# Layer 1's feed-forward output product as seven block products instead of eight

## The chip, the core and the metric

The kernel runs on one core of a Trainium2 chip. The metric is the device time of one launch in microseconds (us), the median of repeated runs. On the core TensorE (PE) multiplies, VectorE (DVE) and ScalarE (ACT) do elementwise work, GpSimd (POOL) a little more, and SyncE (SP) issues the DMAs. Every engine takes its own instructions strictly in the order in which they stand in the program.

## What is computed

A two-layer backbone over 1024 latent tokens and 256 context tokens, in fp32. Layer 0 mixes by a gated convolution and a chunked gate, layer 1 by attention; each ends in a SwiGLU feed-forward part. The change concerns the feed-forward part of layer 1, for the latent tokens:

```
def _swiglu(h, w_in, w_out):
    gt, up = jnp.split(h @ w_in, 2, axis=-1)
    return (jax.nn.silu(gt) * up) @ w_out
x = _post_norm(x, _swiglu(_modulate(x, m_lat[3], m_lat[4]), ffn_w_in[l], ffn_w_out[l]),
               m_lat[5], ln_g[l, 1], ln_b[l, 1])
# _post_norm(x, y, gate, g, b) = _layernorm(ALPHA * x + gate * y, g, b)
# w_in 1024 x 5632, w_out 2816 x 1024; 1024 tokens
```

## The kernel before

A matrix product in fp32 is made of three matmuls (`mm3`, L89 to L92): both operands are split into a rounded part (hi, a cast on ACT, L201) and the rest (lo, a subtraction on DVE, L202), and hi·hi, hi·lo and lo·hi are added up in a PSUM bank. One matmul is 128x128 by 128x512. Its stationary side is called a here, its moving side b.

The feed-forward input product, `ffn_in2` (L547), is a seven-product scheme already: for each of the 22 inner blocks j (128 wide) it makes seven products W[n] by H, four `mm3` each, and combines them on DVE. Its result for block j, two 128x512 tiles `d` and `a` (the two token halves), goes to the DRAM tensor `act_d` (L635, L638). After each second block `step` lets one piece of the background job `bg_ada` run: the adaLN vectors, two loads of `ada_w` and two multiply-adds on DVE (L128) a piece, a sum over partitions on POOL after each fourth.

The output product, `ffn_out2` (L641), is a plain blocked one. Two halves `kb` of 11 inner blocks; in each, for the two output halves h, the weights are loaded and split (`sw` to `w2`, 22 buffers), and with h = 0 the activations come back from `act_d` (`raw`, L656) and are split into `aT`. Then two groups of four token tiles, with the inner block outside and the tile inside, so that four PSUM banks are filled together; only the last group goes tile by tile (`end`). The first half's banks are copied out on ACT (L695); in the second half DVE adds them, multiplies by the gate and adds the residual (L701 to L703, L699). That is 22 x 8 x 2 `mm3`, 1056 matmuls. The end of the program (L1177 to L1186) is a layer norm of the eight token tiles on DVE: two BN_STATS (L208), an aggregate, a power on POOL, two instructions with the mean (L1181), two with the scale (L1184), and the stores.

The order of each engine's instructions is fixed when the program is built: a scheduler plays the program through with its own model of time, and each engine's queue is the order in which things came up there. Buffers (`U`: 61 tiles of 128x512; `w2`: 22; `sw`: 4) are handed out in that order too. All DMAs stand in SP's queue.

## Time and profile before

| | us |
|---|---|
| median of 3 runs | 2629.03 (2627.96 to 2629.47) |
| the profiled execution, whole | 2629.6 |
| its span, first to last instruction | 2627.7 |
| layer 1's `ffn_in2` in the span | about 1952 to 2369 |
| layer 1's `ffn_out2`, first to last matmul | about 2369 to 2608 |
| after the last matmul | 2608 to 2627.7 |

Busy shares over the span: PE 97%, weight loads 81%, DVE 70%, ACT 36%, POOL 12%. The mean granted TensorE clock is 0.987 of full speed. A matmul's own duration in the rows (0.39 us) is longer than the distance to the next one, since matmuls overlap: for PE the distance from start to start counts.

### The profile page before, as it was taken

The page shows a single profiled execution, that of the slowest core. Times are in us where ns is not written, and L with a number is a line of the kernel's source. Part 1 is how long each engine was busy: PE and PEld are TensorE (multiplying, and loading weights), DVE is VectorE, ACT ScalarE, POOL GpSimd, SP SyncE. Part 2 cuts the span into 40 slices and gives each one's busy share as a digit, 9 for nine tenths or more (in the row PEclk, how much of TensorE's full clock was granted, in tenths as well). Part 3 has the DMA queues.
Part 4 walks back from the last instruction along what each step waited for, and adds up shares of the span by engine and source line. Part 5 has one row for each costly group of instructions (what it writes and reads, how often), then busy time and mean ns, then how long its engine had stood idle before and what let it go on. Part 6 is the DMA issues. An engine that isn't in the chain of part 4 may idle for free. (4 is left out here: it accounts for less than half of the span.)

```text
span 2627.7 us, 34744 instructions
## 1 busy us (share of the span) xinstructions
PE 2541.2 (97%) x12956; PEld 2138.1 (81%) x12956; DVE 1851.3 (70%) x3162; ACT 933.4 (36%) x1656; POOL 326.2 (12%) x254
## 2 busy tenths in 40 slices
PE   8999999999999999989999999999989999999997
PEld 6778888787788888879988789888868888888885
DVE  3888488999866655687759488777688665663267
ACT  1311145323233323164433277666163333342220
POOL 0132000112200020010006332222001000000001
PEclk9999999999999999989999999999999999999998
DMA  8453155344422753266541100113324222243232
GB/s 242 144 186 110 57 168 171 118 160 141 129 81 83 268 175 110 91 227 195 183 141 52 41 29 25 65 41 102 131 73 144 81 81 89 80 168 133 68 117 77
DMA packets 156106, 313.68 MB, mean 119 GB/s; under 512 B 25696, under 2 KB 45152, under 8 KB 155936
## 3 DMA queue, kind: packets, MB, share of 16 engines
q1 hardware_dynamic: 155936, 311.46, 36.1%
q8 instruction: 102, 1.67, 0.3%
q14 instruction: 68, 0.56, 0.1%
HBM read 262.05 MB, written 49.35 MB: 119 GB/s over the span
## 5 line engine op out<-in xcount | busy, mean ns | idle before, releaser
L90 PE MATMUL mm<-u,w 128*128 128x512 f32 x1232 | 480.6, 392 | 11.9 <-DVE m L591 4.5
L91 PE MATMUL mm<-u,w 128*128 128x512 f32 x1232 | 482.8, 392 | 3.8 <-DVE u L202 2.8
L92 PE MATMUL mm<-u,w 128*128 128x512 f32 x1232 | 476.7, 391 | 1.9 <-DVE w L202 1.9
L90 PE MATMUL mm<-w,u 128*128 128x512 f32 x832 | 322.7, 392 | 5.8 <-ACT u L201 3.0
L91 PE MATMUL mm<-w,u 128*128 128x512 f32 x832 | 324.3, 390 | 0.0
L92 PE MATMUL mm<-w,u 128*128 128x512 f32 x832 | 321.5, 390 | 0.0
L201 ACT CAST w<-sw 128x512 fp32r<-128x512 f32 x264 | 163.2, 622 | 419.7 <-PE mm L91 365.9
L202 DVE TENSOR_TENSOR w<-sw,w 128x512 fp32r<-128x512 f32 x264 | 191.1, 728 | 169.8 <-ACT w L201 138.5
L90 PEld LDWEIGHTS mm<-u,w 128*128 128x128 f32 x1232 | 232.8, 189 | 64.0 <-DVE m L591 6.4
L91 PEld LDWEIGHTS mm<-u,w 128*128 128x128 f32 x1232 | 232.7, 189 | 53.6 <-DVE u L202 4.6
L92 PEld LDWEIGHTS mm<-u,w 128*128 128x128 f32 x1232 | 232.8, 189 | 50.9 <-DVE w L202 2.6
L90 PE MATMUL mm<-u,hi 128*128 128x256 f32 (+1 forms) x736 | 238.5, 324 | 3.3 <-ACT tt L470 1.8
L84 ACT CAST hi<-wf 128x1024 fp32r<-128x1024 f32 x134 | 138.8, 1050 | 285.3 <-PE mm L91 76.9
L92 PE MATMUL mm<-u,lo 128*128 128x256 f32 (+1 forms) x736 | 237.5, 324 | 0.8 <-DVE lo L86 0.8
L91 PE MATMUL mm<-u,hi 128*128 128x256 f32 (+1 forms) x736 | 237.8, 323 | 0.0
L90 PE MATMUL mm<-hi,u 128*128 128x512 f32 x536 | 209.3, 395 | 3.6 <-DVE tt L917 1.3
L91 PE MATMUL mm<-lo,u 128*128 128x512 f32 x536 | 210.0, 392 | 2.1 <-DVE lo L86 2.1
L92 PE MATMUL mm<-hi,u 128*128 128x512 f32 x536 | 205.7, 393 | 0.0
L86 DVE TENSOR_TENSOR lo<-wf,hi 128x1024 fp32r<-128x1024 f32 x134 | 164.5, 1238 | 43.2 <-ACT hi L84 43.2
L90 PEld LDWEIGHTS mm<-w,u 128*128 128x128 f32 x832 | 157.2, 189 | 39.4 <-ACT u L201 3.9
L92 PEld LDWEIGHTS mm<-w,u 128*128 128x128 f32 x832 | 156.6, 188 | 32.7
L91 PEld LDWEIGHTS mm<-w,u 128*128 128x128 f32 x832 | 156.6, 188 | 32.3
(186 smaller groups left out, 4538.8 us busy)
## 6 DMA issues: line engine op xcount, KB each, us to landing
raw<-in_ffn_in SPq DMA_DIRECT2D x88, 512.0 KB
ad<-in_ada_w SPq DMA_DIRECT2D x112, 256.0 KB
act<-m SPq DMA_DIRECT2D x88, 256.0 KB
raw<-act SPq DMA_DIRECT2D x44, 512.0 KB
sw<-in_ffn_out SPq DMA_DIRECT2D x88, 256.0 KB
wf<-in_ffn_in SPq DMA_DIRECT2D x44, 512.0 KB
wf<-in_w_m SPq DMA_DIRECT2D x32, 512.0 KB
ab<-in_ada_w SPq DMA_DIRECT2D x48, 256.0 KB
```

Of the source, the lines that this page charges most:

```text
L84: nc.scalar.copy(hi, wf)
L86: (lo_eng or nc.vector).tensor_tensor(out=lo, in0=wf, in1=hi.bitcast(F32), op=ALU.subtract)
L90: nc.tensor.matmul(ps, s[0], m[0], start=first, stop=False, skip_group_check=more)
L91: nc.tensor.matmul(ps, s[0], m[1], start=False, stop=False, skip_group_check=more)
L92: return nc.tensor.matmul(ps, s[1], m[0], start=False, stop=last, skip_group_check=more)
L201: nc.scalar.copy(hi, src)
L202: return nc.vector.tensor_tensor(out=lo, in0=src, in1=hi.bitcast(F32), op=ALU.subtract)
```

## The change

`ffn_out2` stays as it is for layer 0. For layer 1 the product is cut once in each of its three directions, as in `ffn_in2`: token halves (tiles 0 to 3, 4 to 7), even and odd inner blocks, output halves. Four block products per output block pair, eight in all, become seven, each of 11 inner blocks by four token tiles: 924 matmuls.

- In `ffn_in2` after each odd block, `out_forms` (new) makes the left sides a of the products out of the two blocks' four tiles (four adds or subtractions, three new tiles from `ad`) and stores seven tiles to DRAM (`fa`), where four went to `act_d`. It also loads the four 128x512 weight tiles of the pair, makes four combined ones (four subtractions) and stores these (`fb`).
- `ffn_out7` (new) runs the products in the order 5, 1, 6, 2, 3, 7, 4. `load` brings a product's 11 left and 11 right tiles and splits each: 154 pairs of a cast and a subtraction, where there were 88. `y`, `x`, `v` and `z` are groups of four banks; 6 and 3 are added onto what `y` holds, 2 onto `x`. Between the products ACT copies banks out (after 5 and 1) or DVE adds and multiplies them, brings in the residual (`xres`) and combines (`more`). `tail` is the layer norm of one tile: tiles 0 to 3 after product 3, tiles 4 to 7 after product 4.
- The eight last pieces of `bg_ada` (layer 1, vector 5) run in layer 0's `ffn_out2` (10 steps a group where there were 8) instead of layer 1's `ffn_in2`.

```diff
--- before.py
+++ after.py
@@ -544,7 +544,7 @@
             sub(F[1, 0, i], F[1, 0, i], F[1, 1, i])
             form(4, F[1, 0, i])
 
-    def ffn_in2(pp, wq, l, H, act_d, steps=0, pre=2):
+    def ffn_in2(pp, wq, l, H, act_d, steps=0, pre=2, forms=None):
         def load_raw(j):
             raw = wq.tile([P, 1024], F32, tag="raw", name="raw", bufs=3)
             nc.sync.dma_start(out=raw, in_=A["ffn_in"][l, j])
@@ -601,6 +601,28 @@
             st["s"] = buf()
             nc.scalar.activation(st["s"], st["x"], AF.Silu)
 
+        def out_forms(q, e, o):
+            fa, fb = forms
+            (a11, a21), (a12, a22) = e, o
+            s3, s2, s4 = (wq.tile([P, 512], F32, tag="ad", name="ad", bufs=4) for _ in range(3))
+            sub(s3, a11, a21)
+            add(a21, a21, a22)
+            sub(s2, a21, a11)
+            sub(s4, a12, s2)
+            for n, f in ((1, a11), (2, a12), (4, a22), (5, a21), (6, s2), (7, s3), (3, s4)):
+                nc.sync.dma_start(out=fa[n][q], in_=f)
+            b11, b12, b21, b22 = (U([P, 512], F32) for _ in range(4))
+            for n, f in enumerate((b11, b12, b21, b22)):
+                nc.sync.dma_start(out=f, in_=A["ffn_out"][l, 2 * q + n // 2, :, (n % 2) * 512:(n % 2 + 1) * 512])
+            sub(b11, b12, b11)
+            sub(b12, b22, b12)
+            sub(b22, b22, b11)
+            sub(b21, b21, b22)
+            for n, f in ((5, b11), (7, b12), (6, b22), (4, b21)):
+                nc.sync.dma_start(out=fb[n][q], in_=f)
+        even = None
         ready = {}
         for j in range(pre):
             ready[j] = {"W": weights1(j)}
@@ -632,10 +654,16 @@
             nc.scalar.activation(c, c, AF.Silu)
             prod(v, W, 4, False, True)
             nc.vector.tensor_tensor(out=d, in0=d, in1=c, op=ALU.mult)
-            nc.sync.dma_start(out=act_d[j, :, 512:1024], in_=d)
+            if forms is None:
+                nc.sync.dma_start(out=act_d[j, :, 512:1024], in_=d)
             add(a, a, v)
             marks["in"] = nc.vector.tensor_tensor(out=a, in0=a, in1=st["s"], op=ALU.mult)
-            nc.sync.dma_start(out=act_d[j, :, 0:512], in_=a)
+            if forms is None:
+                nc.sync.dma_start(out=act_d[j, :, 0:512], in_=a)
+            elif j % 2 == 0:
+                even = (a, d)
+            else:
+                out_forms(j // 2, even, (a, d))
             step(steps if j % 2 else 0)
 
     def ffn_out2(pp, wq, l, act_d, xn, acc, steps=0, hook=None):
@@ -716,6 +744,110 @@
                         if kb == 0:
                             step(steps)
 
+    def ffn_out7(pp, wq, l, forms, xn, acc, tail):
+        fa, fb = forms
+        NP = NJ // 2
+        gate = gate_bc(0, l, 5)
+        g0, g1 = gate[:, 0:512], gate[:, 512:1024]
+        rows = [(ln_row("ln_g", l, 0, h, buf=T), ln_row("ln_b", l, 0, h, buf=T)) for h in range(2)]
+        raw_b = {1: (0, 0), 2: (1, 0), 3: (1, 1)}
+        def tt(out, a, b, op):
+            return nc.vector.tensor_tensor(out=out, in0=a, in1=b, op=op)
+        def xres(t, h):
+            x = U([P, 512], F32)
+            nc.sync.dma_start(out=x, in_=xn[t * P:(t + 1) * P, h * 512:(h + 1) * 512])
+            tt(x, x, rows[h][0], ALU.mult)
+            tt(x, x, rows[h][1], ALU.add)
+            return x
+        def load(n):
+            res = []
+            for k in range(NP):
+                raw = U([P, 512], F32)
+                nc.sync.dma_start(out=raw, in_=fa[n][k])
+                a = (U([P, 512], F32R), U([P, 512], F32R))
+                split(raw, *a)
+                w = wq.tile([P, 512], F32, tag="sw", name="sw", bufs=4)
+                if n in raw_b:
+                    r, h = raw_b[n]
+                    nc.sync.dma_start(out=w, in_=A["ffn_out"][l, 2 * k + r, :, h * 512:(h + 1) * 512])
+                else:
+                    nc.sync.dma_start(out=w, in_=fb[n][k])
+                b = tuple(wq.tile([P, 512], F32R, tag="w2", name="w2", bufs=22) for _ in range(2))
+                split(w, *b)
+                res.append((a, b))
+            return res
+        def one(ps, ab, i, k, first):
+            (hi, lo), b = ab[k]
+            sl = slice(i * P, (i + 1) * P)
+            mm3(ps, (hi[:, sl], lo[:, sl]), b, first and k == 0, k == NP - 1, not first)
+        def run(n, pss, first):
+            ab = load(n)
+            for k in range(NP):
+                for i in range(4):
+                    one(pss[i], ab, i, k, first)
+        def banks(tr):
+            return [pp.tile([P, 512], F32, tag="tr", name="tr", bufs=2) if i < tr else
+                    pp.tile([P, 512], F32, tag="mm", name="mm", bufs=6) for i in range(4)]
+        R = range(4)
+        y = banks(2)
+        run(5, y, True)
+        for i in R:
+            acc[4 + i] = [U([P, 512], F32), U([P, 512], F32)]
+            nc.scalar.copy(acc[4 + i][0], y[i])
+        x = banks(0)
+        run(1, x, True)
+        for i in R:
+            acc[i] = [U([P, 512], F32), U([P, 512], F32)]
+            nc.scalar.copy(acc[i][1], x[i])
+        run(6, y, False)
+        for i in R:
+            tt(acc[4 + i][1], acc[i][1], y[i], ALU.add)
+            tt(acc[4 + i][0], acc[4 + i][1], acc[4 + i][0], ALU.subtract)
+        for i in R:
+            r = xres(i, 1)
+            tt(acc[i][1], acc[i][1], g1, ALU.mult)
+            tt(acc[i][1], acc[i][1], r, ALU.add)
+        run(2, x, False)
+        for i in R:
+            r = xres(i, 0)
+            tt(acc[i][0], g0, x[i], ALU.mult)
+            tt(acc[i][0], acc[i][0], r, ALU.add)
+        for i in R:
+            for h, g in ((0, g0), (1, g1)):
+                r = xres(4 + i, h)
+                tt(acc[4 + i][h], acc[4 + i][h], g, ALU.mult)
+                tt(acc[4 + i][h], acc[4 + i][h], r, ALU.add)
+        def more(t, h, g, ps):
+            m = M2([P, 512])
+            tt(m, g, ps, ALU.mult)
+            tt(acc[t][h], acc[t][h], m, ALU.add)
+        run(3, y, False)
+        for i in R:
+            more(i, 1, g1, y[i])
+            tail(i)
+        v = banks(0)
+        run(7, v, True)
+        for i in R:
+            more(4 + i, 1, g1, v[i])
+            more(4 + i, 0, g0, v[i])
+        z = banks(2)
+        ab = load(4)
+        for i in R:
+            for k in range(NP):
+                one(z[i], ab, i, k, True)
+            more(4 + i, 0, g0, z[i])
+            tail(4 + i)
     def ln_spill(a, t, xn):
         ln_norm(a)
         for h in range(2):
@@ -811,7 +943,7 @@
     so = mod_cols(0, 0, 1, (0, 0))
     hT = None
     xr0_d = dp.tile([SEQ, D], F32, name="xr0_d")
-    act_d = [dp.tile([NJ, P, 1024], F32, name=f"act{l}") for l in range(2)]
+    act_d = [dp.tile([NJ, P, 1024], F32, name=f"act{l}") for l in range(1)]
     H, F = {}, {}
     tiles = [[acc[t] for t in range(4 * g, 4 * g + 4)] for g in range(2)]
     for g in range(2):
@@ -858,8 +990,8 @@
     need(0, 5)
     need(1, 1)
     acc = {}
-    ada_buf.update(ac=singles(T), rd=singles(T), end=72)
-    ffn_out2(pp, wq, 0, act_d[0], xr0_d, acc, steps=8, hook=ctx_ffn_start)
+    ada_buf.update(ac=singles(T), rd=singles(T), end=80)
+    ffn_out2(pp, wq, 0, act_d[0], xr0_d, acc, steps=10, hook=ctx_ffn_start)
     wpF.__exit__(None, None, None)
     WB[:] = [4, 7]
     wpA = tc.tile_pool(name="wpA2", bufs=4, reuse_waits="tile")
@@ -1171,11 +1303,15 @@
 
 
     acc = {}
-    ada_buf.update(ac=UF, rd=UF, end=80)
-    ffn_in2(pp, wq, 1, H, act_d[1], steps=1)
-    ffn_out2(pp, wq, 1, act_d[1], xr1_d, acc)
-    rows = [ln_row(nm, 1, 1, h, scale=False, buf=lambda: U([P, 512], F32)) for nm in ("ln_g", "ln_b") for h in range(2)]
-    for t in range(8):
+    forms = tuple({n: dp.tile([NJ // 2, P, 512], F32, name=f"f{c}{n}") for n in ns}
+                  for c, ns in (("a", range(1, 8)), ("b", range(4, 8))))
+    ffn_in2(pp, wq, 1, H, None, forms=forms)
+    rows = []
+    def tail(t):
+        if not rows:
+            rows.extend(ln_row(nm, 1, 1, h, scale=False, buf=lambda: U([P, 512], F32))
+                        for nm in ("ln_g", "ln_b") for h in range(2))
         mv, rs = ln_stats(acc[t])
         for h in range(2):
             nc.vector.scalar_tensor_tensor(out=acc[t][h], in0=acc[t][h], scalar=mv[:, 0:1], in1=rows[h],
@@ -1184,6 +1320,8 @@
             nc.vector.scalar_tensor_tensor(out=acc[t][h], in0=acc[t][h], scalar=rs[:, 0:1], in1=rows[2 + h],
                                            op0=ALU.mult, op1=ALU.add)
             nc.sync.dma_start(out=out[t * P:(t + 1) * P, h * 512:(h + 1) * 512], in_=acc[t][h])
+    ffn_out7(pp, wq, 1, forms, xr1_d, acc, tail)
     ppC.__exit__(None, None, None)
     wpD.__exit__(None, None, None)
 
```

Where the queues moved. Names: `u` is a tile of the pool `U` (left sides, accumulators, residuals), `w2` a split weight, `sw` a loaded one, `gate` and `tt` rows of constants, `mm` and `tr` PSUM banks; L202 is a split, L757 is any elementwise instruction of `ffn_out7`.

DVE, layer 1, the only place of `ffn_out2` where the left sides change (from the first to the second half of the inner blocks), before: L681 multiplies accumulators by the gate.

```order
L202 TENSOR_TENSOR w_22693<-sw,w_22692 128x512
L681 TENSOR_TENSOR u<-u,gate 128x512 x3
L202 TENSOR_TENSOR w_22709<-sw,w_22708 128x512
L681 TENSOR_TENSOR u<-u,gate 128x512
L202 TENSOR_TENSOR u<-raw,u 128x512 x22
```

DVE now, from product 6 to product 2, the last 11 instructions ahead of the first split of product 2's left sides (`u_22879`):

```order
L757 TENSOR_TENSOR u_22575<-u_22575,gate_22006 128x512
L757 TENSOR_TENSOR u_22852<-u_22852,tt_22014 128x512
L757 TENSOR_TENSOR u_22297<-u_22298,u_22297 128x512
L757 TENSOR_TENSOR u_22578<-u_22578,gate_22006 128x512
L757 TENSOR_TENSOR u_22858<-u_22858,tt_22014 128x512
L757 TENSOR_TENSOR u_22288<-u_22288,gate_22006 128x512
L757 TENSOR_TENSOR u_22289<-u_22289,gate_22006 128x512
L757 TENSOR_TENSOR u_22864<-u_22864,tt_22014 128x512
L757 TENSOR_TENSOR u_22870<-u_22870,tt_22014 128x512
L757 TENSOR_TENSOR u_22291<-u_22291,gate_22006 128x512
L757 TENSOR_TENSOR u_22292<-u_22292,gate_22006 128x512
L202 TENSOR_TENSOR u_22879<-u_22876,u_22878 128x512
```

Ten more stand ahead of these: the four that read product 6's banks, one weight split, five of L757. So 21 instructions stand between the end of product 6 and the first split; five come before the second split (`u_22891`), three before the third.

DVE now, from product 2 to product 3; the first row reads product 2's last bank, the last is the first split of product 3's left sides:

```order
L757 TENSOR_TENSOR u<-gate,mm 128x512
L208 BN_STATS st<-u 128x6
L202 TENSOR_TENSOR w_23341<-sw,w_23340 128x512
L757 TENSOR_TENSOR u<-u,tt 128x512 x7
L757 TENSOR_TENSOR u<-u 128x512
L757 TENSOR_TENSOR u<-u,tt 128x512 x6
L757 TENSOR_TENSOR u<-u 128x512
L757 TENSOR_TENSOR u<-u,tt 128x512 x3
L208 BN_STATS st<-u 128x6
L757 TENSOR_TENSOR u<-u,tt 128x512
L202 TENSOR_TENSOR u<-u 128x512
```

Here 23 instructions stand ahead of the first split, and four each ahead of the second and the third.

DVE at the end of the program, before: L699 multiplies the bank of each of the last four token tiles by the gate, as that tile ends (PE takes them one after the other, 33 matmuls each); layer-norm instructions of other tiles stand between.

```order
L699 TENSOR_TENSOR m_23288<-gate,mm 128x512
L703 TENSOR_TENSOR u<-u,m_23282 128x512
L1184 SCALAR_TENSOR_TENSOR u<-u,rs 128x512 x2
L210 BN_AGGR mv<-st 128x2
L1184 SCALAR_TENSOR_TENSOR u<-u,rs 128x512 x2
L703 TENSOR_TENSOR u<-u,m_23288 128x512
L208 BN_STATS st<-u 128x6
L699 TENSOR_TENSOR m_23294<-gate,mm 128x512
```

DVE at the end of the program now:

```order
L757 TENSOR_TENSOR m_24017<-gate,tr 128x512
L757 TENSOR_TENSOR m_24068<-gate,tr 128x512
L757 TENSOR_TENSOR u<-u,m_24017 128x512
L757 TENSOR_TENSOR m_24119<-gate,mm 128x512
L757 TENSOR_TENSOR u<-u,m_24068 128x512
L757 TENSOR_TENSOR m_24170<-gate,mm 128x512
L208 BN_STATS st<-u 128x6 x2
L757 TENSOR_TENSOR u<-u,m_24119 128x512
L208 BN_STATS st<-u 128x6
L757 TENSOR_TENSOR u<-u,m_24170 128x512
L210 BN_AGGR mv<-st 128x2 x2
L212 TENSOR_SCALAR ve<-mv 128x1
```

In PE's queue product 4 goes inner block by inner block over all four tiles, so that the four banks end within the last nine matmuls. The layer norms of tiles 4 to 7 all stand behind the multiply that reads the last bank (`m_24170`): 33 more instructions, 16 of them SCALAR_TENSOR_TENSOR.

## Rows read from the trace of the kernel before

**Rows 1.** The page: busy us (share) xinstructions of each engine over the span.

```profile
PE 2541.2 (97%) x12956; PEld 2138.1 (81%) x12956; DVE 1851.3 (70%) x3162; ACT 933.4 (36%) x1656; POOL 326.2 (12%) x254
```

**Rows 2.** Stretches: length, PE, PEld, DVE, ACT, POOL busy, clock, DMA share, GB/s.

```profile
1980.00:2370.00 390.00, 390.00 (x1723) 322.92 (x1722) 250.80 (x389) 131.15 (x222) 10.00 (x6) 1.00 0.32 111
2370.00:2400.00 30.00, 30.00 (x134) 24.86 (x133) 11.53 (x19) 5.16 (x9) 0.62 (x1) 1.00 0.37 127
2400.00:2500.00 100.00, 98.48 (x435) 81.23 (x434) 25.27 (x38) 27.24 (x47) 0.00 (x0) 1.00 0.25 82
2500.00:2620.00 120.00, 108.38 (x479) 89.43 (x477) 83.62 (x147) 12.27 (x21) 6.51 (x7) 0.96 0.26 86
```

**Rows 3.** Timeline, PE and ACT, between the halves: start, us, what, [idle before].

```profile
2484.87 1.95 ACT L695 COPY u<-mm 128x512 f32<-128x512 f32 x3 [0.28 <-PE mm L92]
2487.24 0.59 ACT L695 COPY u<-mm 128x512 f32<-128x512 f32 x1
2487.71 3.23 ACT L201 CAST u<-raw 128x512 fp32r<-128x512 f32 x6
2486.49 0.39 PE L92 MATMUL mm<-w,u 128*128 128x512 f32 x1
2488.39 0.50 PE L90 MATMUL mm<-w,u 128*128 128x512 f32 x1 [1.52 <-ACT u L201]
```

**Rows 4.** Timeline of DVE near the end, instructions in a row.

```profile
2577.74 0.69 DVE L702 TENSOR_TENSOR u<-u,gate 128x512 f32<-128x512 f32 x1
...
2582.55 0.69 DVE L208 BATCH_NORM_STATS2 st<-u 128x6 f32<-128x512 f32 x1
...
2615.21 1.40 DVE L1181 SCALAR_TENSOR_TENSOR u<-u,mv 128x512 f32<-128x512 f32 x2
```

**Rows 5.** Groups by line, 2400 to 2628: xcount, busy us, mean ns, idle before.

```profile
L202 DVE TENSOR_TENSOR w<-sw,w 128x512 fp32r<-128x512 f32 x33 | 22.8, 690 | 92.3 <-ACT w L201 92.3
L201 ACT CAST w<-sw 128x512 fp32r<-128x512 f32 x33 | 20.6, 624 | 73.5 <-PE mm L91 70.7 <-DVE m L679 2.1 <-DVE w L202 0.7
```

**Rows 6.** Timeline: the last matmul and DVE's last instructions.

```profile
2607.99 0.39 PE L92 MATMUL mm<-w,u 128*128 128x512 f32 x1
...
2623.21 1.40 DVE L1184 SCALAR_TENSOR_TENSOR u<-u,rs 128x512 f32<-128x512 f32 x2
```

**Rows 7.** The clock: a matmul after an idle time, and stretches as in rows 2.

```profile
699.49 0.50 PE L90 MATMUL mm<-u,w 128*128 128x512 f32 x1 [1.80 <-DVE m L591]
700.00:703.00 3.00, 3.00 (x8) 2.34 (x8) 1.64 (x7) 0.00 (x0) 0.00 (x0) 0.50 0.47 162
706.00:709.00 3.00, 3.00 (x15) 2.48 (x14) 2.85 (x5) 1.39 (x3) 0.00 (x0) 1.00 0.00 0
1950.00:1960.00 10.00, 5.09 (x11) 3.02 (x12) 10.00 (x18) 5.85 (x11) 0.00 (x0) 0.53 0.00 0
2484.00:2488.00 4.00, 2.88 (x13) 2.06 (x11) 3.20 (x5) 3.54 (x7) 0.00 (x0) 1.00 0.33 115
```

**Rows 8.** DMA: a dense stretch; 512 KB loads and the cast that waits for one.

```profile
890.00:905.00 15.00, 15.00 (x67) 12.41 (x67) 13.03 (x21) 5.52 (x10) 0.11 (x1) 1.00 1.03 384
2489.98 9.65 SPq L656 DMA_DIRECT2D raw<-act  x6
2493.43 1.14 ACT L201 CAST u<-raw 128x512 fp32r<-128x512 f32 x2 [2.49 <-DMA raw<-act]
```

**Rows 9.** `ffn_in2` of layer 1: two stretches, and DVE's waits (us, times, longest).

```profile
1970.00:1980.00 10.00, 10.00 (x46) 8.29 (x45) 9.93 (x17) 2.64 (x5) 0.00 (x0) 1.00 0.38 109
2040.00:2060.00 20.00, 20.00 (x90) 16.57 (x89) 11.94 (x19) 6.27 (x11) 0.00 (x0) 1.00 0.25 85
DVE w L202 <- PE mm L91: 35.6, 10, 3.9
```

**Rows 10.** The adaLN multiply-adds in layer 0's `ffn_out2`: ns min/median/max, first and last start.

```profile
L128 DVE SCALAR_TENSOR_TENSOR tt<-ad,sc,tt x48: 741/752/754, 887.2 to 973.7; 128x512 f32<-128x512 f32 x48
```

## The prediction

> **What bounds the kernel now.** I read the page's busy shares first, then the stretches of layer 1's feed-forward part, then PE's waits there, the timeline at the places that the new order changes, and last the clock and the DMA rows. The reader is to see three things. PE is busy 97% of the span [rows 1], and in layer 1's `ffn_in2` all the time: 1723 recorded matmuls in 390 us, one per 0.226 us [rows 2]. In `ffn_out2` it stays so (134 in 30 us) but for one wait of 1.52 us, where the second half of the inner blocks begins and the left sides change: ACT copies four banks out, then makes the first cast, and PE waits for that [rows 3]. DVE and ACT are far from full there (25 and 27 of 100 us [rows 2]). After the last matmul, started at 2607.99, the layer norm on DVE runs on; its last two instructions start at 2623.21 and take 1.40 [rows 6], and the span ends at 2627.7. So PE's work is the bound, then 19.7 us of tail.
>
> **Removed: 132 matmuls.** 1056 become 924. Each takes one distance of 0.226 us: 132 x 0.226 = **-29.9 us**, all on the path. The wait between the halves goes too, **-1.5** [rows 3].
>
> **Added: six changes of product instead of one change of half.** What PE needs first in a product is the cast (ACT) and then the subtraction (DVE) of its left side for inner block 0. Eight matmuls of a block need no subtraction of the left side (8 x 0.226 = 1.8 us); then PE stops for it. One inner block is 12 matmuls, 2.72 us. DVE starts one 128x512 instruction after the other every 0.60 us (2577.74 to 2582.55 holds eight: 4.81 / 8) and the four-operand kind with a scalar every 0.67 (two in 1.40, the last one's own 0.74 in it) [rows 4]. The order shown with the change says how many stand ahead. I take that order as certain and the times as measured.
>
> *5 to 1.* ACT does one copy and one cast of a weight after the product's last matmuls, then the first left cast, as between the halves today: 1.5 there [rows 3], I take **+2.0**, since SP issues the first left tile only once a weight buffer is free. Bounds 1 and 3.
>
> *1 to 6.* All four copies stand directly ahead of the first left cast: 4 x 0.6 + 0.62 = 3.0, less a head start of 0.3 since the first bank ends three matmuls early: **+2.7**. Bounds 1.5 and 4.
>
> *6 to 2.* 21 instructions on DVE between the last matmul of 6 and the first subtraction: 21 x 0.60 + 0.7 = 13.3, and 0.3 for the start: 13.6. PE does 1.8 of work meanwhile: 11.8. The second subtraction is six instructions on, 3.6 us against PE's 2.7: 0.9 more. Together **+12.7**. Nothing covers it, since PE's queue holds only product 2. The bounds: 9 if DVE is ahead by five instructions, 15 at 0.69 each, the duration of a single one [rows 5].
>
> *2 to 3.* 23 stand ahead, of which the first reads the last bank: 23 x 0.60 + 0.7 = 14.5, less 1.8 is 12.7; the second and third subtractions cost 0.3 each, and the residuals' 12 loads (3 MB) come in the same 10 us, for which the densest stretch, 384 GB/s [rows 8], is just enough: **+13.6**. Bounds 10 and 17.
>
> *3 to 7.* Here the first left tile is ready ahead. But through product 7 DVE holds 33 plain instructions, 16 with a scalar and eight short ones (0.1 each): 19.8 + 10.7 + 0.8 = 31.3 us, against 29.9 of PE with a head start of 2. The fifth left tile is the late one: **+2.2**. Bounds 0 and 6.
>
> *7 to 4.* Two left tiles ahead of the evictions, the others one per 0.6 to 3 us behind: **0**.
>
> *The clock.* After 1.80 us of idle the granted clock was 0.50 for some 3 us, and eight matmuls ran where 15 run at full clock; an idle of 1.52 left it at 1.00 [rows 7]. The long idle at 1950 to 1960 had 0.53 over ten us [rows 7]. So a stop costs about 1.6 us of half speed behind it (3.4 us x 7/15). At 6 to 2 and 2 to 3 part of that lies inside DVE's delay. I take **+4** for four stops; bounds 0 and 9.
>
> [...] Rows 5 show 690 ns for one subtraction, rows 4 a start every 0.60 us. [...]
>
> **The tail.** Today the last four tiles end one by one, and their layer norms are already between [rows 6]: 19.7 us from the last matmul's start. In the new order 34 instructions stand from the last bank's multiply on: ten plain (6.0), 16 with a scalar (10.7), eight short (0.8), 0.5 for a wait on POOL, and the three that are queued ahead delay the start by 1.1 behind the usual 0.5. That is 19.6, and the way from DVE's last end (2624.6) to the span's end, 3.1: 22.7, so **+3.0**. Bounds -2 and +6. Tiles 0 to 3 have their layer norm earlier, but it is DVE's work in product 7.
>
> **Added in `ffn_in2`:** 88 subtractions and adds, 88 x 0.60 = 53 us of DVE in 390, of which it is idle 139 [rows 2]; the sixteen multiply-adds of the adaLN job leave (12 us). DVE now waits for PE to free weight buffers [rows 9], so it is ahead, and PE's matmuls cover it. The tight place is the start: DVE is busy 9.93 of 10 us at 1970, but 60% from 2040 on [rows 9]. DMA: 15 transfers of 256 KB a pair of blocks replace four, 2.9 MB more in 38 us, to 111 GB/s add 76. SP's queue is held by stores that wait for DVE; the weight loads stand behind them, with some blocks of reserve. **0**, bounds 0 and 6.
>
> **Moved: eight pieces of the adaLN job,** 16 multiply-adds of 0.75 us [rows 10], 16 loads, two sums on POOL, into layer 0's `ffn_out2`. There they end some 29 us later than the 974 of now, ahead of the change of half. The DMA queue passes them before the second half's weights. **0**, bounds 0 and 2.
>
> DMA in the new output product: 170 tiles of 256 KB, 44.6 MB in some 240 us, 186 GB/s, below the 384 of rows 8. A 512 KB load is used at most 3.45 us after its issue [rows 8]; the left tiles are issued three inner blocks (8 us) ahead.
>
> **The sum.** -29.9 - 1.5 + 2.0 + 2.7 + 12.7 + 13.6 + 2.2 + 4 + 3.0 = **+8.8 us**. The profiled execution took 2629.6, the median of the runs is 2629.03; on the median that is 2637.8, so **2638 us**. All low bounds together would give -12, all high ones +37; they are independent, so I take the forecast's own range as 2622 to 2656.
>
> **The rivals.**
>
> *The matmuls' price alone comes through (faster).* Place: the changes 6 to 2 and 2 to 3. For them to be hidden, DVE must have the first left tiles split before the banks are read. Against it: an engine takes its queue in order, and the first split stands behind them. For it: 17 of the 21 need no bank, and I may misjudge how late their operands are; the case decides for faster once the two stops cost less than half (13 us instead of 26). With stops like the one of today [rows 3], 1.5 to 2.7 each: -29.9 - 1.5 + 4 x 2 + 2 + 3 = -18 to -25, about **2608**. [...] Chance 0.15.
>
> *The block loop is paced by something else throughout (slower still).* Each of 77 inner blocks needs two loads, two casts and two subtractions in 2.72 us; casts take 1.25 and subtractions 1.38 [rows 5], each waiting for the other and for a buffer that PE frees. If the loop of load, cast, split, matmul runs 0.3 us over, that is 77 x 0.3 = 23 more: **2661**. It decides from a landing later than about 6 us. Against it: rows 8. Chance 0.10.
>
> *The change only moves the bound and comes out even.* Stops of 9 and 10, no clock loss: **2629**; this is inside the forecast's range.
>
> **How the numbers follow.** A kernel like this repeats within 0.1%, so 0.2%, 5.3 us, is what can be told from no change: same is 2623.8 to 2634.3. The forecast has 0.75, of which two thirds lie above 2634.3 and most of the rest within the band; with the rivals: slower 0.59, same 0.21, faster 0.20. Range 2617 to 2656: it leaves out the faster rival's centre (0.1 below) and the paced loop (0.1 above).
>
> **What would show it.** Right: PE's idle time in layer 1's output product, 1.5 us today, becomes some 30 in two stops of 11 to 14 us that DVE's L202 ends, and two of 2 to 3 that ACT's L201 ends; 0.50 clock behind them; 924 matmuls; the last matmul about 3 us further from the end. Wrong: stops ended by DMA, or none; PE idle in `ffn_in2`; a stop at 1010 to 1040 in layer 0's `ffn_out2`.

## The result

The changed kernel takes **2664.64 us** (median of four runs, 2663.99 to 2666.69) against 2628.49 for the kernel before (four runs, 2627.11 to 2629.47): a ratio of 1.0139, 95% interval 1.0122 to 1.0157. It is slower by 36 us, where 9 were forecast, and outside the range. The profiled execution took 2664.95 us, its span is 2663.2, 35.5 longer than before.

The page's busy line after (busy us, share of the span, instructions), to be read beside [rows 1]:

```profile
PE 2528.6 (95%) x12824; PEld 2121.2 (80%) x12824; DVE 1955.0 (73%) x3336; ACT 964.6 (36%) x1714; POOL 327.2 (12%) x254
```

132 matmuls are gone and PE is less busy, by 12.6 us only, since matmuls at half clock (0.50 granted from 1023 to 1027) stay busy longer (0.79 us for the first one behind the stop in the rows below, 0.50 behind one at full clock in [rows 3]). The waits say more. PE's waits after, first in layer 1's input product (1985 to 2400 us), where the kernel before has none, then in the output product (2365 to 2663), where it has the 1.52 us of [rows 3] alone: what waits for what, us in total, times, longest.

```profile
PE mm L90 <- DVE m L591: 9.0, 4, 3.6
```

```profile
PE tr L90 <- ACT u L201: 13.6, 2, 11.0
PE mm L90 <- ACT u L201: 8.9, 2, 6.4
PE mm L92 <- DVE u L202: 6.2, 4, 2.7
PE tr L92 <- DVE u L202: 1.3, 1, 1.3
```

The third place is outside layer 1's feed-forward part. Timeline of layer 0's output product at its change of half (start, us, what, idle before and what ended it), from five engines; before, PE waited 1.52 us at this place as well:

```profile
1001.53 3.54 POOL L134 PARTITION_ALL_REDUCE tt<-tt  x1 [10.12 <-DVE tt L128]
...
1012.94 3.85 POOL L227 TENSOR_SCALAR tt<-tt 128x512 f32<-128x512 f32 x4 [7.87 <-issue]
1013.59 4.34 DVE L706 TENSOR_TENSOR m<-m,tt 128x512 f32<-128x512 f32 x5 [8.97 <-POOL tt L227]
...
1019.15 6.95 SPq L692 DMA_DIRECT2D sw<-in_ffn_out  x5
...
1022.06 0.62 ACT L201 CAST w<-sw 128x512 fp32r<-128x512 f32 x1 [8.56 <-DMA sw<-in_ffn_out]
1023.74 0.79 PE L90 MATMUL mm<-w,u 128*128 128x512 f32 x1 [10.18 <-ACT u L201]
```

This is read from the bottom up. PE waits for the first left cast; on ACT a weight's cast stands ahead of it and waits for its load; SP issues that load only when DVE has freed a buffer, after a wait of 12.8 us; DVE stands at L706, the residual, whose scaled rows come from POOL; and POOL does them after the last sum of the adaLN job, which the change has put there.

The matmul starts give the price of each place, idle time and half clock together: the time from one start to the next less 0.2267 us per matmul.

| place | idle, us | with half clock, us | forecast, us |
|---|---|---|---|
| 132 matmuls fewer | | -29.9 | -29.9 |
| the wait between the halves, gone | -1.5 | -1.8 | -1.5 |
| 5 to 1 | 2.5 | 4.4 | +2.0 |
| 1 to 6 | 2.6 | 4.5 | +2.7 |
| 6 to 2 | 8.9 | 12.7 | +12.7 |
| 2 to 3 | 12.3 | 14.7 | +13.6 |
| product 7 | 3.6 | 6.8 | +2.2 |
| clock, all of these | | in the rows above | +4 |
| tail (22.2 after the last matmul's start, 19.7 before) | | +2.5 | +3.0 |
| layer 1's input product | 9.0 | +13.2 | 0 |
| layer 0's change of half | 8.7 more | +11.1 | 0 |

The column sums to 38.2. The stretch between layer 0's output product and layer 1's input product gives 2.8 back, which was not assigned to anything; together that is the 35.5 of the span but for 0.1.

### The profile page after: what moved, and what is told of

Read it like the earlier page. It is cut to its first block, busy times and chain, and to the rows that moved or that the text cites. A ratio compares the mean times of both kernels' runs of the same rounds, so it can differ in the third digit from the quotient of the medians.

```text
span 2663.2 us, 35221 instructions
## 1 busy us (share of the span) xinstructions
PE 2528.6 (95%) x12824; PEld 2121.2 (80%) x12824; DVE 1955.0 (73%) x3336; ACT 964.6 (36%) x1714; POOL 327.2 (12%) x254
## 4 chain that ended last, share of the span: by engine, by line
PE 48%; DVE 7%; DMA 4%; ACT 3%; issue 2%; POOL 1%; SPq 0%; DVEq 0%; ACTq 0%; POOLq 0%
PE mm L90 13%; PE mm L91 13%; PE mm L92 13%; PE tr L91 2%; PE tr L90 2%; PE tr L92 2%; PE tr L1179 2%; DVE u L757 1%; POOL tt L134 1%; DMA ad<-in_ada_w 1%; ACT pt L1164 1%; DVE u L202 1%; PE sa L90 1%; PE sa L91 1%; PE sa L92 1%
## 5 line engine op out<-in xcount | busy, mean ns | idle before, releaser
L90 PE MATMUL mm<-u,w 128*128 128x512 f32 x1232 | 481.1, 393 | 20.8 <-DVE m L591 13.6
L92 PE MATMUL mm<-u,w 128*128 128x512 f32 x1232 | 477.9, 392 | 1.9 <-DVE w L202 1.9
L201 ACT CAST w<-sw 128x512 fp32r<-128x512 f32 x297 | 182.8, 621 | 438.9 <-PE mm L91 394.8
L90 PE MATMUL mm<-w,u 128*128 128x512 f32 x700 | 276.9, 399 | 21.9 <-ACT u L201 19.1
L90 PEld LDWEIGHTS mm<-u,w 128*128 128x128 f32 x1232 | 232.9, 189 | 74.9 <-DVE m L591 17.4
L202 DVE TENSOR_TENSOR w<-sw,w 128x512 fp32r<-128x512 f32 x297 | 214.9, 728 | 93.7 <-ACT w L201 69.0
L91 PE MATMUL mm<-w,u 128*128 128x512 f32 x700 | 277.8, 397 | 0.0
L92 PEld LDWEIGHTS mm<-u,w 128*128 128x128 f32 x1232 | 233.1, 189 | 51.0 <-DVE w L202 2.6
L92 PE MATMUL mm<-w,u 128*128 128x512 f32 x700 | 258.0, 394 | 6.2 <-DVE u L202 6.2
L90 PE MATMUL mm<-u,hi 128*128 128x256 f32 (+1 forms) x736 | 238.6, 324 | 3.2 <-ACT tt L470 2.3
L92 PE MATMUL mm<-u,lo 128*128 128x256 f32 (+1 forms) x736 | 237.4, 324 | 0.5 <-DVE lo L86 0.5
L90 PE MATMUL mm<-hi,u 128*128 128x512 f32 x536 | 209.9, 396 | 3.5 <-ACT u L192 1.3
L92 PE MATMUL mm<-hi,u 128*128 128x512 f32 x536 | 206.2, 394 | 0.0
L90 PEld LDWEIGHTS mm<-w,u 128*128 128x128 f32 x700 | 134.9, 193 | 52.5 <-ACT u L201 20.9
L201 ACT CAST w<-raw 128x512 fp32r<-128x512 f32 x148 | 90.4, 621 | 231.1 <-PE mm L91 209.8
L92 PEld LDWEIGHTS mm<-w,u 128*128 128x128 f32 x700 | 132.6, 190 | 35.6 <-DVE u L202 8.2
```

Source lines behind the costliest of these rows:

```text
L90: nc.tensor.matmul(ps, s[0], m[0], start=first, stop=False, skip_group_check=more)
L91: nc.tensor.matmul(ps, s[0], m[1], start=False, stop=False, skip_group_check=more)
L92: return nc.tensor.matmul(ps, s[1], m[0], start=False, stop=last, skip_group_check=more)
L201: nc.scalar.copy(hi, src)
L202: return nc.vector.tensor_tensor(out=lo, in0=src, in1=hi.bitcast(F32), op=ALU.subtract)
```

## The experiments

Each is compared by its ratio to runs of the kernel before on the same chip, 2624.4 to 2624.9 us there; a change of 0.2% is 5 us. They go by place, and the last two take everything together.

### Layer 0: the moved job alone

```diff
-    ada_buf.update(ac=singles(T), rd=singles(T), end=72)
-    ffn_out2(pp, wq, 0, act_d[0], xr0_d, acc, steps=8, hook=ctx_ffn_start)
+    ada_buf.update(ac=singles(T), rd=singles(T), end=80)
+    ffn_out2(pp, wq, 0, act_d[0], xr0_d, acc, steps=10, hook=ctx_ffn_start)
-    ffn_in2(pp, wq, 1, H, act_d[1], steps=1)
+    ffn_in2(pp, wq, 1, H, act_d[1])
```

(on the kernel before, without its `end=80` line in layer 1)

> The kernel before with one part of the change alone: the last eight pieces of the adaLN job run in layer 0's output product (ten steps a group instead of eight) and none in layer 1's input product. Theory A (the moved job alone makes the 10.2 us stop at the half boundary of layer 0, because its sums on POOL push the scaling of the residual rows back, DVE stands behind that, and the weight splits and loads behind DVE): PE waits about 10 us at that place instead of 1.5, and with the half clock behind it the time rises by 9 to 11 us, to 2638 to 2640. Rival (the stop needs something else of the changed kernel, or the move is free as the prediction had it): 1.5 us there and 2627 to 2631.

Measured: 1.0039 (1.0024 to 1.0054), 10 us, and 10.38 us of idle at that place:

```profile
1023.28 0.80 PE L90 MATMUL mm<-w,u 128*128 128x512 f32 x1 [10.38 <-ACT u L201]
```

The move alone makes the stop, in a kernel with no seven-product output at all.

Undone in the changed kernel (the same lines the other way):

> The changed kernel with the adaLN pieces back where they were (eight steps a group in layer 0's output product, the last eight pieces in layer 1's input product). Theory A (the move costs layer 0 its 10 us stop): 1.5 us there, the first matmul of layer 1's input product about 8 to 10 us earlier, 1.0100 to 1.0110 of the kernel before if nothing is added in layer 1. Rival (the move was needed: its loads add to a queue of SP that is already full at the start of layer 1's input product): the waits on L591 there grow by as much, 1.013 to 1.015.

Measured: 1.0081 (1.0067 to 1.0094), 15 us better than with the move; 1.52 us at the change of half, and 4.4 us of idle in layer 1's input product where there were 9.0. The pieces did no harm there, so the rival falls; that they did some good, beyond what was expected, is not explained.

Then which part of the job's chain it is:

```diff
-            nc.gpsimd.tensor_scalar(out=t, in0=t, scalar1=ALPHA, scalar2=1.0, op0=ALU.mult, op1=ALU.mult)
+            (eng or nc.gpsimd).tensor_scalar(out=t, in0=t, scalar1=ALPHA, scalar2=1.0, op0=ALU.mult, op1=ALU.mult)
...
-                    rg, rb = ln_row("ln_g", l, 0, h, buf=T), ln_row("ln_b", l, 0, h, buf=T)
+                    rg, rb = ln_row("ln_g", l, 0, h, buf=T, eng=nc.vector), ln_row("ln_b", l, 0, h, buf=T, eng=nc.vector)
```

> The changed kernel with one edit in layer 0's output product: the four residual rows are scaled on DVE (0.6 to 0.7 us each) instead of on POOL. Theory P (POOL is part of the chain that makes the 10.2 us stop: after the job's last sum it starts the scaling only 7.9 us later, and that takes 3.9): DVE begins the residual at about 1009 instead of 1013.6, the stop becomes 4 to 6 us, 1.011 to 1.012 of the kernel before. Rival B (the rows' loads themselves come late, since the moved job holds the buffers until 1005): DVE begins only when the last row has landed, a stop of 8 us or more, 1.013 or more.

Measured: 1.0120 (1.0105 to 1.0135), 5 us better than the changed kernel. The job stays moved, and the stop is 2.46 us, less than either side expected. Timeline of DVE and PE there, the rows now scaled on DVE:

```profile
1001.48 0.50 DVE L227 TENSOR_SCALAR tt<-tt 128x512 f32<-128x512 f32 x1 [1.88 <-DMA tt<-in_ln_g]
1002.01 2.50 DVE L706 TENSOR_TENSOR m<-m,tt 128x512 f32<-128x512 f32 x4
```

```profile
1014.04 0.80 PE L90 MATMUL mm<-w,u 128*128 128x512 f32 x1 [2.46 <-ACT u L201]
```

DVE begins the residual at 1002.0 instead of 1013.6. The loads were late by little (DVE waited 1.88 us for one). The rest is POOL's: its last sum, which runs to 1005.1, and the 7.87 us between that sum and the scaling.

### Layer 1's input product: when the right sides are made

```diff
-                nc.sync.dma_start(out=f, in_=A["ffn_out"][l, ...])
+                i1 = nc.sync.dma_start(out=f, in_=A["ffn_out"][l, ...])
+                after(i1, [marks["in"]])
```

> The changed kernel with one edit: the loads of the right sides of a pair of blocks are placed behind that pair's last product in layer 1's input product, so that they come spread over 390 us instead of all in the first 130. Theory A (the 9.0 us of PE waits and 4 us of half clock in the input product come from SP's queue being filled with right-side loads and stores ahead of the next weights): the four waits on the add of L591 go, 13 us less, about 2652. Rival (the work itself, 88 more instructions on DVE and 15 transfers a pair, is what costs; where it stands does not matter): waits of the same sum elsewhere in the stage, 2662 to 2666.

Measured: 1.0167 (1.0152 to 1.0182), 7 us slower than the changed kernel. Yet the four waits are gone but for one of 0.8 us at the stage's end. What came in their place is 13.9 us of idle in the output product's first blocks, 11.24 of them at 2376, at its first matmul: the last pair's transfers stood on SP ahead of product 5's first left tile. With the half clock the stage gains 12 us and those blocks lose 16. So the theory held for the place and failed for the sum, since the edit had its own bill. A second run spreads the pairs so that they end at block 15:

```diff
+        def right_forms(q):
+            fa, fb = forms
             b11, b12, b21, b22 = (U([P, 512], F32) for _ in range(4))
...
                 out_forms(j // 2, even, (a, d))
+            if forms is not None and j in (0, 2, 3, 5, 6, 8, 9, 11, 12, 14, 15):
+                right_forms((0, 2, 3, 5, 6, 8, 9, 11, 12, 14, 15).index(j))
```

> The changed kernel with the right sides taken out of the pair's step and loaded one pair after each of blocks 0, 2, 3, 5, 6, 8, 9, 11, 12, 14 and 15 of layer 1's input product, so neither all at the start nor one at the very end. Theory A (the waits of the input product come from SP's queue being filled with right-side transfers at the start; with one pair per pair of blocks they went, but the last pair then came 11 us late for the first product): no wait over 1 us in the input product after its start, no stop at the start of the output product, 11 to 14 us less than the changed kernel, about 1.0085 to 1.0095 of the kernel before. Rival (transfers and 53 us of extra DVE work cost the same wherever they stand): 1.0125 or more.

Measured: 1.0103 (1.0088 to 1.0118), 9 us better, a little less than expected. PE does not wait in the stage after its start, nor at 2376. The same work, DVE's 53 us and all transfers, is in both kernels; the stretches from 1990 to 2130 and from 2130 to 2360 differ in when it is done (columns as in [rows 2]). The changed kernel, then the one with the right sides spread:

```profile
1990.00:2130.00 140.00, 130.98 (x561) 106.83 (x560) 108.17 (x177) 38.62 (x69) 0.00 (x0) 0.98 0.75 256
2130.00:2360.00 230.00, 230.00 (x1016) 190.46 (x1015) 156.68 (x247) 72.81 (x122) 0.00 (x0) 1.00 0.31 107
```

```profile
1990.00:2130.00 140.00, 140.00 (x620) 115.95 (x619) 106.98 (x170) 44.07 (x75) 0.00 (x0) 1.00 0.55 189
2130.00:2360.00 230.00, 230.00 (x1017) 190.50 (x1016) 166.92 (x265) 74.42 (x125) 0.00 (x0) 1.00 0.47 161
```

DVE's waits in 1990 to 2130 name the mechanism. In the changed kernel, from 1985 on:

```profile
DVE u L523 <- DMA u<-in_ffn_out: 15.4, 9, 3.6
DVE sw L570 <- DMA raw<-in_ffn_in: 14.6, 5, 4.5
```

With the right sides spread:

```profile
DVE sw L570 <- DMA raw<-in_ffn_in: 9.7, 7, 3.7
...
DVE u L523 <- DMA u<-in_ffn_out: 0.7, 3, 0.3
```

A right-side tile has no reason to wait for a block, so the scheduler put all 44 loads and stores into 137 us of the stage's 428, from 1975 on. There DVE, in order, stood 15.4 us at subtractions whose tiles had not landed, and the add that frees PE's bank (L591) stood behind. Whether the tiles were late by SP's order or by the rate, 256 GB/s where it was 94, was not separated.

### The stops between the products: DVE's queue or the loads

The trace after contradicts the prediction at the largest stop. From product 2 to 3:

```profile
2528.92 4.76 SPq L761 DMA_DIRECT2D u<-xr_d  x10
...
2534.02 0.32 SPq L770 DMA_DIRECT2D u<-fa  x1
...
2540.40 0.62 ACT L201 CAST u<-u 128x512 fp32r<-128x512 f32 x1 [9.88 <-DMA u<-fa]
2541.07 0.79 PE L90 MATMUL tr<-w,u 128*128 128x512 f32 x1 [10.98 <-ACT u L201]
...
2545.26 0.68 DVE L202 TENSOR_TENSOR u<-u 128x512 fp32r<-128x512 f32 x1
2546.00 0.73 PE L92 MATMUL tr<-w,u 128*128 128x512 f32 x2 [1.32 <-DVE u L202]
```

The stop of 10.98 us ends with ACT's cast, not with DVE's subtraction: the first left tile is issued behind ten residual loads and lands 6.4 us after its issue. The DMA engines are busy 0.99 of that time, so the tile waits for data already on the way, and not for SP alone (columns as in [rows 2]):

```profile
2530.00:2540.00 10.00, 0.09 (x1) 0.00 (x0) 10.00 (x18) 0.52 (x1) 0.00 (x0) 0.71 0.99 342
```

DVE's queue, the prediction's cause, costs only the 1.32 behind it. Two runs take one of the two away each. Both leave part of the residual out: the first scales it not at all, the second does not load it. Each ran once, and only its waits are read.

```diff
             nc.sync.dma_start(out=x, in_=xn[...])
-            tt(x, x, rows[h][0], ALU.mult)
-            tt(x, x, rows[h][1], ALU.add)
             return x
```

> The changed kernel without the scaling of the residual (the two row instructions on DVE, 32 in all, are left out; its 16 loads stay). At 2 to 3, 14 instead of 23 instructions stand on DVE ahead of the first left split. Theory D (the prediction's: the stop is made by DVE's queue): the stop of 11.0 us becomes about 5.5 (nine instructions less at 0.60). Rival L (the first left tile is loaded behind twelve residual loads on SP, and the stop ends with its cast): the stop stays 10 to 11 us, and only the later waits on DVE go.

```diff
-            nc.sync.dma_start(out=x, in_=xn[...])
-            tt(x, x, rows[h][0], ALU.mult)
+            tt(x, rows[h][1], rows[h][0], ALU.mult)
             tt(x, x, rows[h][1], ALU.add)
```

> The changed kernel without the residual's 16 loads (the row instructions stay and work on constant rows instead of the residual). At 2 to 3, 13 instructions stand on DVE ahead of the first left split, about as many as in the run that keeps the loads and leaves the row instructions out. Theory D (DVE's queue makes the stop): about 5.5 us, as there. Rival L (the loads ahead of the first left tile make it): 2 to 3 us until the first cast, then a wait for DVE of 3 us at the first lo matmul.

Measured, PE's waits at 2 to 3. Without the scaling, with DVE's last residual adds and the cast:

```profile
2533.03 2.72 DVE L757 TENSOR_TENSOR u<-u 128x512 f32<-128x512 f32 x4 [0.31 <-DMA u<-xr_d]
2535.80 0.62 ACT L201 CAST u<-u 128x512 fp32r<-128x512 f32 x1 [10.15 <-DVE u L757]
2536.47 0.79 PE L90 MATMUL tr<-w,u 128*128 128x512 f32 x1 [11.25 <-ACT u L201]
```

Without the loads, with the first left subtraction on DVE:

```profile
2525.24 0.50 PE L90 MATMUL tr<-w,u 128*128 128x512 f32 x1 [2.99 <-ACT u L201]
2534.55 1.22 PE L92 MATMUL tr<-w,u 128*128 128x512 f32 x2 [7.21 <-DVE u L202]
```

```profile
2525.41 0.68 DVE L757 TENSOR_TENSOR u<-gate,mm 128x512 f32<-128x512 f32 x1
...
2533.82 0.68 DVE L202 TENSOR_TENSOR u<-u 128x512 fp32r<-128x512 f32 x1
```

Nine instructions fewer on DVE leave the stop as it was, 11.25 against 10.98, and take the 1.32 behind it away. The profile puts the cast here down to a DVE add; but these adds wait for the residual's loads themselves, and by the trace's semaphore events the left tile landed at 2535.72, within 0.1 us of the last add's end, so the loads alone would have kept PE as long. Without the loads the first wait is 2.99, as the loads' side expected, but 7.21 of DVE's queue appear behind it, more than its 3: DVE comes to the last bank's read only at 2525.41. There are two chains, of nearly the same length, and each alone is worth some 10 us. Theory D has the wrong chain and rival L half of the truth. (In the last two rows 14 starts lie 8.41 us apart: 0.60 each, the prediction's price.)

Both chains come from the order in which the work is written. So that order was turned:

```diff
-        run(6, y, False)
+        run(ab, y, False)
+        ab = load(2)
         for i in R:
             tt(acc[4 + i][1], acc[i][1], y[i], ALU.add)
```

(and the like at each product: the next product's loads and splits stand ahead of the work on this one's banks)

> The changed kernel with one edit in the output product: the loads and splits of a product's tiles are written ahead of the copies, multiplies and residual work of the product before it, so that on DVE the first left splits stand ahead of the bank reads. Theory A (the stops between the products are made by the order on DVE and SP alone; no bank is needed again until two products later): the 35 us of excess at 5 to 1, 1 to 6, 6 to 2 and 2 to 3 shrink to under 5, about 2630 to 2634; the last products, where DVE is full, keep theirs. Rival (DMA bounds it: the residual's loads and the left tiles compete, so that left tiles land late in any order): half stays, 2645 to 2650.

Measured: 1.0061 (1.0046 to 1.0076), 20 us better. PE's waits in the output product, 30.0 us in the changed kernel:

```profile
PE tr L92 <- DVE u L202: 6.0, 2, 5.1
PE mm L90 <- ACT u L201: 5.1, 1, 5.1
PE mm L92 <- DVE u L202: 3.4, 2, 2.9
```

14.5 us. The changes 5 to 1, 1 to 6 and 6 to 2 are free. What is left has moved one change on, since the work was only put behind the next product's tiles: 5.1 us at the first block of product 3, where the work on product 6's banks and its residual stands on DVE ahead of the left split; 5.1 at 3 to 7, where the twelve residual loads stand on SP ahead of product 7's first left tile; and the rest in products 7 and 4. So three changes went as the theory has it, but the 20 us are the rival's price (15 to 20 less, where the theory has 31 to 35): about half of the idle time stays. The residual was then moved to products 1 and 6:

```diff
+        res = {(i, h): xres(i, h) for i in R for h in range(2)}
         ab = load(6)
...
-            r = xres(i, 1)
+            r = res[i, 1]
```

> The kernel with the loads first and one more edit: the residual tiles of all eight token tiles are loaded and scaled during products 1 and 6, where DVE is half idle, instead of at 6 to 2 and 2 to 3. Theory A (what is left of the stops, 5.1 us inside product 2 and 5.1 and 2.9 inside product 3, is DVE and SP held by the residual's work in front of later left tiles): these go, 12 to 15 us with the half clock, to about 1.001 of the kernel before. Rival (the loads of the left tiles are late for want of buffers, and early residuals take 16 more of them): the stops move to products 1 and 6 and keep their sum, 1.005 to 1.008.

(The expectation names the three places one product too early; they are those of the paragraph above it.)

Measured: 1.0042 (1.0028 to 1.0056), 5 us better, hardly clear of the two intervals. The idle time is 1.6 us less (12.9 in all, in waits of 4.0, 3.1 and less), 4.0 with the half clock, and the tail 3.4 less (19.5 against 22.9). That is the rival's side: eight residual loads in a row on SP make a 4.0 us stop at 6 to 2, where twelve had made 5.1 at 3 to 7, and the first block of product 3 still waits 3.1 for DVE.

### The tail

```diff
-        for i in R:
+        prev = None
+        for grp in ((0, 1), (2,), (3,)):
             for k in range(NP):
-                one(z[i], ab, i, k, True)
...
+                for i in grp:
+                    n0, last = one(z[i], ab, i, k, True)
+                    if prev is not None:
+                        after(n0, [prev])
+            prev = last
...
```

(`one` now returns its first and its last matmul, and `more` and `tail` follow for the tiles of each group)

> The changed kernel with one edit: PE takes the last product as tiles 4 and 5 together, then tile 6, then tile 7, instead of all four block by block. Theory A (the tail of 22.2 us after the last matmul is the layer norm of four tiles behind the last bank): about 14 instructions instead of 34 stand behind the last bank, the tail is 10 to 12 us, the whole 2653 to 2655. Rival (DVE has not split the last left tiles of the product when the first two tiles want them, 15 us into it instead of 30): PE stops there for what the tail gains, 2662 to 2668.

Measured: 1.0105 (1.0088 to 1.0122), 9 us better. After the last matmul's start 9.4 us are left. DVE at the end of the changed kernel, then of this one:

```profile
2639.57 1.28 DVE L757 TENSOR_TENSOR m<-gate,tr 128x512 f32<-128x512 f32 x2 [10.84 <-PE tr L92]
...
2657.20 2.73 DVE L1320 SCALAR_TENSOR_TENSOR u<-u,rs 128x512 f32<-128x512 f32 x4
```

```profile
2637.34 0.68 DVE L757 TENSOR_TENSOR m<-gate,mm 128x512 f32<-128x512 f32 x1
...
2641.68 1.41 DVE L1328 SCALAR_TENSOR_TENSOR u<-u,rs 128x512 f32<-128x512 f32 x2
```

In the changed kernel DVE stands idle for 10.84 us and then has four layer norms to do; here those of the other three tiles are done but for one instruction. The rival is there too, with a smaller price: PE waits four times, 4.2 us together, for left splits at the start of the product.

### Everything together

One kernel has the job back, the right sides spread, the loads first, one residual tile per inner block of products 5 and 1, and the last product as two tiles, one and one.

> All the edits that helped in one kernel: adaLN pieces back, right sides spread over the blocks, loads first, residual tiles one per inner block of products 5 and 1, last product as two tiles, one and one. Theory A (each place that was found costs what it cost alone, and they add up: 9 in layer 0, 9 to 13 in the input product, 20 to 30 between the products, 10 in the tail): 60 us below the changed kernel, about 0.990 of the kernel before (0.987 to 0.993), with 15 to 20 us of the matmuls' 30 still lost in products 2, 3, 7 and 4, where DVE is full. Rival (DVE and DMA bind the new output product, and what is taken away in one place comes back in the next): 0.998 to 1.004.

Measured: **0.9946** (0.9933 to 0.9960), 2611.06 us against 2624.87: 14 us faster than the kernel before and 51 below the changed one. The single edits add to 59 (15 + 9 + 26 + 9). PE's waits in the output product (its matmuls are written out there: L794 and L796 are what L90 and L92 were):

```profile
PE tr L796 <- DVE u L202: 10.6, 6, 3.1
PE tr L794 <- ACT u L201: 3.7, 1, 3.7
PE mm L794 <- ACT u L201: 0.4, 2, 0.2
```

With the half clock that is 26 us of the matmuls' 30: one stop for a left tile at 1 to 6, and DVE in products 3 and 4. It is busy 42.36 of 48 us from 2480 on, and 48.70 of 52 from 2528.

```profile
2480.00:2528.00 48.00, 43.54 (x178) 33.63 (x177) 42.36 (x71) 17.85 (x31) 0.00 (x0) 0.96 0.53 174
2528.00:2580.00 52.00, 45.50 (x178) 35.17 (x177) 48.70 (x87) 19.08 (x32) 3.00 (x4) 0.90 0.62 203
```

The last run takes three tiles and one in the last product, `for grp in ((0, 1, 2), (3,))`:

> The kernel with all edits, but PE takes the last product as three tiles together and then one, instead of two, one and one. Theory A (in the last product PE runs ahead of DVE's left splits: with two tiles together a block lasts 1.4 us, about what two splits take, with three 2.0): the 12 us of excess in product 4 fall to 5 or less, the tail grows from 9.4 to 13 or 14 us, together 0.992 to 0.994. Rival (DVE is bound over the last two products by its number of instructions in any order): what PE gains the tail loses, 0.9945 as before.

Measured: 0.9961 (0.9947 to 0.9975). The excess of product 4 falls from 12.1 to 8.4 us, the tail grows from 9.4 to 16.1. The tail loses more than PE gains there, so in all it is the rival's outcome, no gain. That DVE bounds the last two products fits this and its 48.70 busy us of 52; no run with less work on DVE there was made.

## Why the prediction was wrong

**Right:** the direction, the 132 matmuls' price, the wait between the halves, the tail (+2.5, forecast +3.0), and the sum over the changes of product: 30.0 us of idle against 33.2. The stops lie where it put them, 1 to 6 at 2.59 against 2.7.

**The step "moved: eight pieces, 0" failed, by 11 us.** It asked whether the job itself ends ahead of the change of half (it does, the last sum at 1005) and whether its DMAs pass. It did not go on to what stands behind the job on POOL, the scaling of the residual rows, nor from there to DVE, SP and ACT. Its own last part named a stop at 1010 to 1040 as the sign that it was wrong, and that is where it was. The moved job alone gave all of it.

**The step "added in `ffn_in2`, 0" failed, by 13 us.** The instructions and bytes were counted right, and spread over the stage they cost no wait at all. The step took a mean (76 GB/s added to 111, DVE idle for 139 of 390 us, [rows 2]) for work that the queues hold in the first third. The prediction read the order of the queues for the output product only, and not here.

**6 to 2 and 2 to 3: the sum right, the mechanism half right.** The prediction let DVE's queue alone make the stops. It asked of the twelve residual loads only whether the rate suffices for them; they stand on SP ahead of the left tile, which lands behind them, and that chain ended last. The DVE chain behind it is real, as the run without the loads shows; one hid the other, so the size was right by two causes of the same length, and that is luck.

**The clock: +4 against some 10.** In the changed kernel's output product the half clock lies behind each of the six idle times of 2.5 us or more, and costs 1.6 to 1.7 us behind each (from the second matmul on, starts 0.43 us apart instead of 0.23). That is the prediction's price; its four stops left out the second wait at 6 to 2 (2.56) and the one in product 7 (2.69), and it took some 2 us off for DVE's delay. The length of an idle time alone does not decide it: in the run without the residual's loads half clock follows an idle time of 2.30 (starts 0.43 us apart behind it) and not one of 2.99 (0.23). (For the 1.52 that left the clock at 1.00, the row of 2484 to 2488 in [rows 7] ends too early; the 1.00 of 2400 to 2500 in [rows 2] shows it.) Here PE after the stop of 6.38 us (columns as in [rows 2]), eight matmuls in 10 us:

```profile
2490.00:2500.00 10.00, 3.78 (x8) 2.48 (x8) 10.00 (x17) 3.60 (x7) 0.00 (x0) 0.50 0.67 245
```

**The rivals.** The paced loop gave nearly the measured time, 2661, but it did not happen: within a product no block waits for loads, casts or splits save at the places above. The faster rival, the matmuls' price alone, needed the stops at 6 to 2 and 2 to 3 to cost less than 13 us together; they cost 27.4, and the 30 us did not come through. PE's weight loads fell from 2138 [rows 1] to 2121 us and the time rose by 36: the engine with the most work got less of it, and what was added made it wait.

## What to carry over

A step that is moved, or added where an engine has idle time, is priced by the order of every queue it enters: what stands behind it there, and who waits for that, two or three engines on. Work that depends on nothing is not spread by itself; here the scheduler put it at the front of the stage, and a mean over the stage says nothing about it. And where two chains of the same length make a stop, taking one away shows nothing, so both are to be looked for before a cause is named; writing the next product's loads ahead of this one's evictions took both at three of the changes, and moved about half of the idle time on to the later ones.

## What the hardware showed

POOL stood idle for 7.87 us between the end of its last sum (1005.1) and the first scaling of a row (1012.94), and the profile shows nothing that it waited for. It was 7.72 us in the kernel before and 7.68 with the moved job alone; in the changed kernel a MEMSET behind a sum starts 0.1 us before that sum's recorded end (950.41, behind 947.00 and 3.54). The kernel before has this pause too, 27 us earlier (985.59), where it costs nothing: PE's wait at that change of half is the 1.52. What fills the pause was not shown.
